# One block of a streaming encoder on one core: attention with ScalarE and VectorE in program order, takes set aside between the scores and Exp, other filler shares and weights loaded further ahead

## The chip, the core and the metric

The kernel runs on one core of one Trainium2 chip. The core has five engines that run their own instruction streams: TensorE (PE; its weight loads are shown apart as PEld), VectorE (DVE), ScalarE (ACT), GpSimd (POOL) and SyncE (SP, which here only issues DMA transfers). The metric is the device time of one launch in microseconds.

## The reference, cut to what matters

```python
D_MODEL = 1024; SEQ = 1024; ATT_HEADS = 8; ATT_HEAD_DIM = 64
CHUNK = 64; LEFT_CHUNKS = 8          # own chunk and 8 chunks before it
def mixer(h, ...):
    proj = h @ w_in
    q, k, v, xr, yr, g_att, g_rec = jnp.split(proj, idx, axis=-1)
    att = chunked_attention(q, k, v, rel_bias) @ w_att_o
    xr = causal_depthwise_conv(xr, conv_w, conv_b)
    rec = (rg_lru(xr, ...) * jax.nn.gelu(yr)) @ w_rec_o
    merged = jax.nn.sigmoid(g_att) * att + jax.nn.sigmoid(g_rec) * rec
    return merged @ w_out
def chunked_attention(q, k, v, rel_bias):   # per head, per chunk of queries
    scores = einsum(q, k_band) * 64**-0.5 + bias[rel]   # invalid keys masked
    return einsum(softmax(scores), v_band)
x = sandwich(x, ffn1, ...); x = sandwich(x, mix, ...); x = sandwich(x, ffn2, ...)
```

The block is a feed-forward half, this mixer and a second feed-forward half. Everything is float32. The kernel gets float32 products from three products of rounded parts: a value is split into a high part (`wh`, `k1h`) and the remainder (`wl`, `k1l`), and high × high, low × high and high × low are summed.

## The kernel before, in words

Only the attention stage matters here; it runs from about 1046 to 1361 us of the profiled span, between the recurrent branch and the merge. Its work is 64 units, in this order: four pairs of heads, two heads each, eight blocks of 128 queries. We call them unit 0 to 63. A unit's window has one to five blocks of 128 keys: in each head, the first query block sees one, the next two, and from the fifth on five. So units 0, 8, 16, ... are the narrow ones.

A unit goes through these steps (lines of the kernel before):

- S, the scores: PE writes a window of up to 640 columns into PSUM (two products up to 512 columns, L1675; four when it is wider, L1681).
- VectorE adds the bias and takes the row maximum in one instruction (L1686), then negates it (`nmx`, L1689). ScalarE does Exp with the row sum (L1690), VectorE the reciprocal (`ri`, L1691), ScalarE the division, a multiplication by `ri` (L1692).
- T, the transposes: PE turns the probabilities (`ptr`, L1700). ScalarE copies the high part out of PSUM (`tt`, L1704), VectorE makes the low part (L1705).
- V, the values: PE multiplies by v (`pvo`, L1718). After every second unit ScalarE and VectorE take the result out: o copy (L1728), two adds (L1729, L1730), `atth` (L1731) and `attl` (L1732).

PE's order is written out by hand: in step i come S of unit i+1, half of the step's filler, V of unit i−1, T of unit i, and the other half of the filler. In the text, "after unit n's scores" means that step. A filler is a product of a projection that is needed later: while pair p is worked on, q and k of pair p+1 are projected (`pproj`, L1552, 24 products of 512 tokens for each half of the tokens), the second half of v (`vproj`, L1616), and the attention's gate (`g_att`, 48 products for 128 channels, with tanh at L1633 and a store to memory). `GATES` says how many gate blocks each pair gets. `SHARE` says how much filler a unit gets by its window's width, and `begin` turns the weight of a pair's fillers into a rate.

A block of a projection, 24 products (48 for v), ends in one PSUM bank. Projections use two banks in turn (`psM`, bufs=2), so block n+2 may only start when what was taken out of block n has been read. These "takes" are left in a list, `left`, and `settle` runs them off later:

- q: ScalarE copies a scaled high part (L1575) and VectorE makes the difference (L1576), once for each of the two heads.
- k: ScalarE casts `k0h` (L1591), VectorE makes `k0l` (L1592), ScalarE casts the other half of `k0h` (L1596), and the same for `k1h`, `k1l`.
- v: ScalarE copies the high part (L1623), VectorE the difference (L1624). A gate: one tanh on ScalarE.

Before, only PE is in written order inside the attention. A scheduler orders ScalarE's and VectorE's instructions by when it estimates that they can run. `settle()` stands three times in each step and takes one item; when a block of a projection ends, `settle(99)` empties the list. Weights come by SP's DMA queue as `raw`, are cast by ScalarE to `wh` (L151), and GpSimd makes `wl`; they are prepared one unit of the plan ahead (`Weights(specs, ahead=1)`).

Of the kernel before, what the change touches and what calls it, by code (L numbers as in the profile page):

```python
# [23 lines left out]
P = 128  # L24
# [14 lines left out]
SHARE = (3, 4, 4, 5, 5)  # L39
LEFT = 40.0  # L40
GATES = (2, 0, 2, 4)
# [7 lines left out]
def kernel(  # L49
# [1449 lines left out]
    def att_phase(hh, hl, wts0, tg_dram, n_ga):  # L1499
        att_h, att_l = [], []  # L1500
        with (
# [11 lines left out]
            def v_w(half, i):  # L1513
                c0 = C_V + half * 256
                return prep(
                    w_in[i * 512 : (i + 1) * 512, c0 : c0 + 256].rearrange("(k p) n -> p k n", p=P), [P, 4, 256], nc.gpsimd
                )

            specs = {("v", 0, 0): partial(v_w, 0, 0), ("v", 0, 1): partial(v_w, 0, 1)}

            def spec_qk(p):
                specs["q", p] = partial(prep_cols, w_in, C_Q + p * P, eng=nc.gpsimd)
                specs["k", p] = partial(prep_cols, w_in, C_K + p * P, eng=nc.gpsimd)

            def spec_ga(n):
                specs["ga", n] = partial(prep_cols, w_in, C_GA + n * P, eng=nc.gpsimd)

# [6 lines left out]
            for p in range(4):  # L1534
                for kind, n in plan[p]:
                    if kind == "qk":
                        spec_qk(n)
                    elif kind == "ga":
                        spec_ga(n)
                    else:  # L1540
                        specs["v", 1, 0] = partial(v_w, 1, 0)
                        specs["v", 1, 1] = partial(v_w, 1, 1)
            wts = Weights(specs, ahead=1)

# [15 lines left out]

            def settle(n=1):
                for _ in range(min(n, len(left))):
                    left.pop(0)()

            def qk(p, out_t):
# [3 lines left out]
                for sh in range(2):  # L1569
                    sl = slice(sh * 512, (sh + 1) * 512)  # L1570
                    pj = yield from pproj(src["q", p], sh)
                    settle(99)

# [10 lines left out]
                for sh in range(2):  # L1584
                    sl = slice(sh * 512, (sh + 1) * 512)
                    pj = yield from pproj(src["k", p], sh)
                    settle(99)

# [15 lines left out]
            def vproj(half, out_t):  # L1604
                vt = []
                for sp in range(4):
                    settle(99)
                    pv = bank("pv")
                    for j in range(2):
                        tk = slice((2 * sp + j) * P, (2 * sp + j + 1) * P)  # L1610
                        dst = pv[:, j * 256 : (j + 1) * 256]
                        for k in range(KB):
                            wh, wl = wts["v", half, k // 4]
                            kk = k % 4
                            for i, (a, b) in enumerate(((hh, wh), (hh, wl), (hl, wh))):
                                nc.tensor.matmul(  # L1616
                                    dst, a[k][:, tk], b[:, kk, :], start=k == 0 and i == 0, stop=k == KB - 1 and i == 2
                                )
                                yield 0.5
                    t = t4("vt", F32R)  # L1620
                    t5 = t.rearrange("p (a q d) -> p a q d", q=4, d=HD)
                    src = pv.rearrange("p (a i d) -> p a i d", i=2, d=HD)
                    nc.scalar.copy(t5[:, :, 0::3, :], src)  # L1623
                    nc.vector.tensor_tensor(t5[:, :, 1:3, :], src, t5[:, :, 0::3, :].bitcast(F32), op=ALU.subtract)  # L1624
                    vt.append(t)
                out_t[half] = vt

            def g_att(n):
                for sh in range(2):
                    pj = yield from pproj(wts["ga", n], sh)  # L1630
                    settle(99)
                    tg = tmp[0].tile([P, 512], F32, tag="v", bufs=1, name=nm("tga"))
                    nc.scalar.activation(tg, pj, AF.Tanh, scale=0.5)  # L1633
                    nc.sync.dma_start(tg_dram[n * P : (n + 1) * P, sh * 512 : (sh + 1) * 512], tg)
                    yield 1.0
# [24 lines left out]
            def scores(u):  # L1660
# [27 lines left out]
                )  # L1688
                nc.vector.tensor_scalar(nmx, mx, -1.0, None, op0=ALU.mult)  # L1689
                nc.scalar.activation(pe[:, :w], pe[:, :w], AF.Exp, bias=nmx, accum_out=sm)  # L1690
                nc.vector.reciprocal(ri, sm)  # L1691
                nc.scalar.activation(pe[:, :w], pe[:, :w], AF.Copy, scale=ri)  # L1692
                return pe

            def probs_t(u, pe):
# [3 lines left out]
                for i in range(nk):  # L1699
                    nc.tensor.transpose(pt[:, i * P : (i + 1) * P], pe[:, i * P : (i + 1) * P], ident)  # L1700
                tt = tmp[0].tile([P, 5, 2, P], F32R, tag="tt", bufs=2, name=nm("tt"))
                src = pt[:, :w].rearrange("p (b n) -> p b n", n=P)
                hi, lo = tt[:, :nk, 0, :], tt[:, :nk, 1, :]
                nc.scalar.copy(hi, src)  # L1704
                nc.vector.tensor_tensor(lo, src, hi.bitcast(F32), op=ALU.subtract)  # L1705
                return tt

            def values(u, tt):
# [8 lines left out]
                for i in range(nk):  # L1717
                    nc.tensor.matmul(  # L1718
                        dst, vslice(p, h, kb0 + i), tt[:, i, :, :].rearrange("p a n -> p (a n)"),
                        start=i == 0, stop=i == nk - 1,  # L1720
                    )
                if qb % 2 == 1:
                    ah, al = atts[p]
# [5 lines left out]
                    nc.vector.tensor_tensor(o32[own], o32[own], pv[own, :, 0, :], op=ALU.add)  # L1729
                    nc.vector.tensor_tensor(o32[own], o32[own], pv[own, :, 1, :], op=ALU.add)  # L1730
                    nc.scalar.copy(ah[own, cols], of[own])  # L1731
                    nc.vector.tensor_tensor(al[own, cols], of[own], ah[own, cols].bitcast(F32), op=ALU.subtract)  # L1732

            def filler(p):
# [10 lines left out]

            with tc.manual_schedule(engines={PE_ENGINE}):
                load_bias(0)
                for _ in qk(0, qkt):
                    pass
                settle(99)  # L1750
                pe_next = scores(units[0])
                for _ in vproj(0, vts):
                    pass
                prev = None
# [11 lines left out]
                def drain():  # L1766
# [3 lines left out]
                    credit = 0.0  # L1770
                    settle(99)
# [8 lines left out]
                for i, u in enumerate(units):  # L1780
                    share = rate * SHARE[window(u[2])[1] - 1]
                    if i + 1 < len(units):
                        n = units[i + 1]
                        if n[1] == 0 and n[2] == 0:
                            drain()
                        pe_after = scores(n)
                        if n[1] == 0 and n[2] == 0:
# [7 lines left out]
                    settle()  # L1795
                    pe_next = pe_after
                    fill(share * 0.5)
                fill(LEFT * 0.4)
                values(*prev)
                drain()  # L1800
# [574 lines left out]
```

## Time and profile before

| | us |
|---|---|
| median of three runs | 2141.08 (2138.83 to 2143.11) |
| profiled execution, its own time | 2139.32 |
| its span in the trace | 2137.5 |
| PE busy | 2109.2, 99% of the span |
| DVE busy | 1393.7, 65% |
| ACT busy | 1049.2, 49% |
| attention: 1046 to 1361 | 315.00, PE busy 309.56 of it |

A line of an instruction group reads: line, engine, operation, output tile <- input tiles, shapes, number of instructions | busy us in all, mean ns of one | idle us of the engine just before them, and what ended most of it. A line of waits reads: the waiting engine, tile and line, what ended the wait, then the total in us, the number of waits and the longest.

### The profile page before, as it was taken

The page shows a single profiled execution, that of the slowest core. Times are in us where ns is not written, and L with a number is a line of the kernel's source. Part 1 is how long each engine was busy: PE and PEld are TensorE (multiplying, and loading weights), DVE is VectorE, ACT ScalarE, POOL GpSimd, SP SyncE. Part 2 cuts the span into 40 slices and gives each one's busy share as a digit, 9 for nine tenths or more (in the row PEclk, how much of TensorE's full clock was granted, in tenths as well). Part 3 has the DMA queues.
Part 4 walks back from the last instruction along what each step waited for, and adds up shares of the span by engine and source line. Part 5 has one row for each costly group of instructions (what it writes and reads, how often), then busy time and mean ns, then how long its engine had stood idle before and what let it go on. Part 6 is the DMA issues. An engine that isn't in the chain of part 4 may idle for free.

```text
span 2137.5 us, 26970 instructions
## 1 busy us (share of the span) xinstructions
PE 2109.2 (99%) x9877; PEld 1749.1 (82%) x9877; DVE 1393.7 (65%) x1878; ACT 1049.2 (49%) x1672; POOL 667.9 (31%) x490
## 2 busy tenths in 40 slices
PE   7999999999999999999999999999999999999998
PEld 5888888888888878888898888888888888888877
DVE  7766886567667687787346666586776655546466
ACT  5433333334357687854357777446343333334443
POOL 1168985422104110100122110002088874422102
PEclk9999999999999999999999999999999999999999
DMA  9457774469776232447611113457167653449465
GB/s 324 115 183 260 262 254 150 128 227 350 279 255 209 73 112 91 136 140 276 238 46 56 46 43 110 148 201 257 65 209 263 236 202 109 128 171 325 164 225 188
DMA packets 263085, 387.74 MB, mean 181 GB/s; under 512 B 17920, under 2 KB 163496, under 8 KB 262952
## 3 DMA queue, kind: packets, MB, share of 16 engines
q1 hardware_dynamic: 250032, 339.79, 47.5%
q10 hardware_dynamic: 12920, 46.23, 5.6%
q8 instruction: 77, 1.26, 0.2%
q14 instruction: 56, 0.46, 0.1%
HBM read 280.58 MB, written 108.52 MB: 182 GB/s over the span
## 4 chain that ended last, share of the span: by engine, by line
PE 87%; DVE 6%; ACT 3%; DMA 2%; issue 1%; SPq 1%; POOL 0%; DVEq 0%; ACTq 0%; POOLq 0%
PE px L992 10%; PE pv L992 8%; PE pj L1552 7%; PE pj L508 6%; PE psX L730 6%; PE psX L731 6%; PE psX L732 6%; PE pj L509 6%; PE pj L510 6%; PE psZ L731 3%; PE psZ L730 3%; PE psZ L732 3%; PE px L1412 2%; PE pv L1616 2%; PE px L1899 2%; PE psY L731 1%
## 5 line engine op out<-in xcount | busy, mean ns | idle before, releaser
L151 ACT CAST dh<-rawd 128x1024 fp32r<-128x1024 f32 x154 | 160.5, 1053 | 202.2 <-PE pv L992 54.0
L721 DVE TENSOR_TENSOR wm<-raw,wm 128x512 fp32r<-128x512 f32 x152 | 163.7, 1080 | 134.3 <-ACT wm L720 129.3
L154 DVE TENSOR_TENSOR dh<-rawd,dh 128x1024 fp32r<-128x1024 f32 x130 | 164.7, 1271 | 124.5 <-ACT dh L151 122.1
L508 PE MATMUL pj<-hh,wh 128*128 128x512 f32 x546 | 215.2, 394 | 0.0
L509 PE MATMUL pj<-hl,wh 128*128 128x512 f32 x546 | 212.8, 390 | 0.0
L510 PE MATMUL pj<-hh,wl 128*128 128x512 f32 x546 | 212.8, 390 | 0.0
L992 PE MATMUL px<-dh,dh 128*128 128x512 f32 x608 | 187.5, 390 | 1.4 <-DVE dh L154 1.4
L992 PE MATMUL pv<-dh,dh 128*128 128x512 f32 x528 | 162.7, 389 | 0.0
L154 POOL TENSOR_TENSOR wl<-raw,wh 128x1024 fp32r<-128x1024 f32 x20 | 48.3, 2422 | 295.4 <-ACT wh L151 249.8
L992 PE MATMUL px<-dh 128*128 128x512 f32 x352 | 137.7, 391 | 0.2 <-ACT dh L151 0.2
L930 POOL TENSOR_TENSOR act<-act,act 128x512 f32<-128x512 f32 x54 | 86.5, 1602 | 160.8 <-DMA act<-act 113.9
L992 PEld LDWEIGHTS px<-dh,dh 128*128 128x128 f32 x608 | 114.0, 188 | 25.8 <-DVE dh L154 2.1
L508 PEld LDWEIGHTS pj<-hh,wh 128*128 128x128 f32 x546 | 102.5, 188 | 23.5 <-issue 1.8
L510 PEld LDWEIGHTS pj<-hh,wl 128*128 128x128 f32 x546 | 102.5, 188 | 21.5
L509 PEld LDWEIGHTS pj<-hl,wh 128*128 128x128 f32 x546 | 102.6, 188 | 20.7 <-DVE hl L364 0.3
L992 PEld LDWEIGHTS pv<-dh,dh 128*128 128x128 f32 x528 | 98.9, 188 | 21.1 <-DVE dh L154 0.7
L730 PE MATMUL psX<-hs,wm 128*128 128x512 f32 x296 | 115.5, 390 | 0.1
L730 PE MATMUL psX<-hh,wm 128*128 128x512 f32 x296 | 115.3, 389 | 0.1
L732 PE MATMUL psX<-hs,wm 128*128 128x512 f32 x296 | 115.2, 389 | 0.0
L731 PE MATMUL psX<-hs,wm 128*128 128x512 f32 x296 | 115.2, 389 | 0.0
L732 PE MATMUL psX<-hh,wm 128*128 128x512 f32 x296 | 115.2, 389 | 0.0
L731 PE MATMUL psX<-hl,wm 128*128 128x512 f32 x296 | 115.1, 389 | 0.0
(362 smaller groups left out, 5485.8 us busy)
## 6 DMA issues: line engine op xcount, KB each, us to landing
rawa<-in_w_ada_dram SPq DMA_DIRECT2D x56, 512.0 KB, 6.5
rawd<-acts SPq DMA_DIRECT2D x88, 256.0 KB, 4.4
rawd<-downs SPq DMA_DIRECT2D x88, 256.0 KB, 5.0
raw<-in_w_in_dram SPq DMA_DIRECT2D x44, 512.0 KB, 4.0
raw<-in_ffn_w_gu_dram SPq DMA_DIRECT2D x43, 512.0 KB, 5.4
sr<-in_ffn_w_gu_dram SPq DMA_DIRECT2D x39, 512.0 KB, 6.3
act<-act SPq DMA_DIRECT2D x37, 512.0 KB, 5.5
acts<-act ACTq DMA_DIRECT2D x36, 512.0 KB, 4.0
```

Of the source, the lines that this page charges most:

```text
L151: nc.scalar.copy(hi, raw)
L154: (eng or nc.vector).tensor_tensor(lo, raw, hi.bitcast(F32), op=ALU.subtract)
L508: nc.tensor.matmul(dst, wh[:, kk, :], xhk[:, sl], start=first, stop=False)
L509: nc.tensor.matmul(dst, wh[:, kk, :], xlk[:, sl], start=False, stop=False)
L510: nc.tensor.matmul(dst, wl[:, kk, :], xhk[:, sl], start=False, stop=last)
L721: nc.vector.tensor_tensor(t[:, 1], src, t[:, 0].bitcast(F32), op=ALU.subtract)
L730: nc.tensor.matmul(dst, t[:, 0, kk, :], xh, start=first and kk == 0, stop=False, skip_group_check=True)
L731: nc.tensor.matmul(dst, t[:, 0, kk, :], xl, start=False, stop=False, skip_group_check=True)
L732: nc.tensor.matmul(dst, t[:, 1, kk, :], xh, start=False, stop=last and kk == 3, skip_group_check=True)
L930: nc.gpsimd.tensor_tensor(o, p, q, op=op)
L992: nc.tensor.matmul(dst, a_[:, 0, tk], w_[:, 1, :], start=first and n == 0, stop=last and n == 2, skip_group_check=True,)
L1552: nc.tensor.matmul(d, a[:, k, :], b[k][:, sl], start=k == 0 and i == 0, stop=k == KB - 1 and i == 2)
```

## The change

ScalarE and VectorE join PE in written order during attention. The code therefore says where each of their instructions goes:

- `aside` stands between `nmx` and Exp of the unit whose scores were just issued. It runs off up to three items of `left` for windows of more than three blocks, else two. A weight cast that is due takes the place of two of them.
- What is still in the list goes when the next block of a projection ends (`settle()` is now "all").
- The takes of v and the tanh of a gate go into `left` too; before, they ran as the block ended.
- The division is a generator step (`divide`): `ri`, and the division itself behind the high part of the transposes. The transposes' low part and the values' two halves are steps as well.
- The class `Queued` loads the weights of the unit four ahead in the plan and casts those two ahead.
- `LEFT`, the filler kept for the end, falls from 40 to 18, and `begin` divides by another total: pairs 1 and 2 no longer leave out one unit's share.

```diff
-LEFT = 40.0
+LEFT = 18.0
...
+            class Queued:
...
+                def load(self, n):
+                    while self.loaded < min(n, len(self.order)):
+                        key = self.order[self.loaded]
+                        src, shape = specs[key]
+                        raw = self.raws[key] = wpool.tile(shape, F32, tag="raw", bufs=3, name=nm("raw"))
+                        nc.sync.dma_start(raw, src.rearrange("(k p) n -> p k n", p=P))
+                        self.loaded += 1
...
+                def __getitem__(self, key):
+                    n = self.order.index(key)
+                    if n > self.asked:
+                        self.asked = n
+                        self.load(n + 4)
+                        for k in self.order[: n + 1]:
+                            self.cut(k)
+                        if n + 2 < len(self.order):
+                            casts.append((step[0] + 1, partial(self.cut, self.order[n + 2])))
+                    return self.got[key]
...
-            def settle(n=1):
+            def settle(n=99):
                 for _ in range(min(n, len(left))):
                     left.pop(0)()
+
+            def aside(n):
+                if casts and casts[0][0] <= step[0]:
+                    casts.pop(0)[1]()
+                    n -= 2
+                settle(max(n, 0))
...
                 nc.vector.tensor_scalar(nmx, mx, -1.0, None, op0=ALU.mult)
+                aside(3 if nk > 3 else 2)
                 nc.scalar.activation(pe[:, :w], pe[:, :w], AF.Exp, bias=nmx, accum_out=sm)
+                return pe, w, sm, ri
+
+            def divide(got):
+                pe, w, sm, ri = got
                 nc.vector.reciprocal(ri, sm)
+                yield
                 nc.scalar.activation(pe[:, :w], pe[:, :w], AF.Copy, scale=ri)
-                return pe
+                yield
...
-            with tc.manual_schedule(engines={PE_ENGINE}):
+            with tc.manual_schedule(engines={PE_ENGINE, mybir.EngineType.DVE, mybir.EngineType.Activation}):
...
-                    tot = sum(SHARE[window(b)[1] - 1] for b in range(SB)) * 2 - SHARE[4]
+                    tot = sum(SHARE[window(b)[1] - 1] for b in range(SB)) * 2 + {0: -SHARE[4], 3: SHARE[4]}.get(p, 0)
...
+                        got = scores(n)
+                        after = divide(got)
...
                     fill(share * 0.5)
+                    out_ = iter(())
                     if prev is not None:
-                        values(*prev)
-                    settle()
-                    prev = (u, probs_t(u, pe_next))
-                    settle()
-                    pe_next = pe_after
+                        out_ = values(*prev)
+                        next(out_)
+                    turned = probs_t(u, pe)
+                    next(turned)
+                    if after:
+                        next(after)
+                    next(out_, None)
+                    next(turned)
+                    tt = next(turned)
+                    if after:
+                        next(after)
+                    next(out_, None)
+                    prev = (u, tt)
                     fill(share * 0.5)
```

Where the instructions go shows in the order in which each engine gets them. In these rows a number behind a name tells tiles apart; the text ahead says which unit is meant. Line numbers of the changed kernel are higher by some 40 to 60.

ScalarE, before, around unit 24: the k casts of the second half of pair 2's k (`pj_1600_9798`), whose bank the second v block needs. `pe_1628` is unit 24, `pe_1611` unit 23.

```order
L1591 CAST k0h_1580_9713<-pj_1600_9798 64x512
L1692 ACTIVATE pe_1611_9854<-pe_1611_9854,ri_1615_9862 128x640
L1704 CAST tt_1618_9896<-ptr_1617_9890 128x5x128
L1731 CAST atth_1561_9638<-o32_1616_9881 64x256
L1596 CAST k0h_1580_9713<-pj_1600_9798 64x512
L1591 CAST k1h_1582_9715<-pj_1600_9798 64x512
L1690 ACTIVATE pe_1628_9937,sm_1631_9942<-pe_1628_9937,nmx_1630_9941 128x128
L1596 CAST k1h_1582_9715<-pj_1600_9798 64x512
```

ScalarE, after: the same casts (bank `pj_1610_9819`). `pe_1650` is unit 26, `pe_1639` unit 25.

```order
L1750 ACTIVATE pe_1639_9975<-pe_1639_9975,ri_1643_9981 128x256
L1793 CAST atth_1565_9643<-o32_1647_10005 64x256
L1635 CAST k0h_1584_9719<-pj_1610_9819 64x512
L1640 CAST k0h_1584_9719<-pj_1610_9819 64x512
L1743 ACTIVATE pe_1650_10024,sm_1653_10029<-pe_1650_10024,nmx_1652_10028 128x384
L1635 CAST k1h_1586_9721<-pj_1610_9819 64x512
L1640 CAST k1h_1586_9721<-pj_1610_9819 64x512
L1763 CAST tt_1659_10061<-ptr_1658_10057 128x2x128
```

The casts that stood around unit 24's Exp now stand around unit 26's. VectorE at these two places, before:

```order
L1592 TENSOR_TENSOR k0l_1581_9714<-pj_1600_9798,k0h_1580_9713 64x512
L1730 TENSOR_TENSOR o32_1616_9881<-o32_1616_9881,pvo_1607_9827 64x256
L1686 ISA pe_1628_9937,mx_1629_9940<-sc_1627_9936,bw_1528_9524 128x128
L1686 ISA mx_1629_9940 128x1
L1705 TENSOR_TENSOR tt_1618_9896<-ptr_1617_9890,tt_1618_9896 128x5x128
L1732 TENSOR_TENSOR attl_1562_9639<-o32_1616_9881,atth_1561_9638 64x256
L1689 TENSOR_SCALAR nmx_1630_9941<-mx_1629_9940 128x1
L1592 TENSOR_TENSOR k1l_1583_9716<-pj_1600_9798,k1h_1582_9715 64x512
```

and after:

```order
L1794 TENSOR_TENSOR attl_1566_9644<-o32_1647_10005,atth_1565_9643 64x256
L1738 ISA pe_1650_10024,mx_1651_10027<-sc_1649_10023,bw_1532_9532 128x384
L1738 ISA mx_1651_10027 128x1
L1741 TENSOR_SCALAR nmx_1652_10028<-mx_1651_10027 128x1
L1636 TENSOR_TENSOR k0l_1585_9720<-pj_1610_9819,k0h_1584_9719 64x512
L1636 TENSOR_TENSOR k1l_1587_9722<-pj_1610_9819,k1h_1586_9721 64x512
L1748 RECIPROCAL ri_1654_10030<-sm_1653_10029 128x1
```

Both low parts of k now stand behind unit 26's bias-and-maximum (`L1738 ISA`) and `nmx`. PE after these scores of unit 26 (`sc_1649`), after the change; `pv_1656` is the second v block, which goes into the bank of `pj_1610`:

```order
L1727 MATMUL sc_1649_10023<-k1l_1418_9009,q1_1372_8847 128x384
L1659 MATMUL pv_1623_9904<-wh_1599_9761,hh_166_966 128x256
L1659 MATMUL pv_1623_9904<-wl_1600_9762,hh_166_966 128x256
L1659 MATMUL pv_1623_9904<-wh_1599_9761,hl_174_974 128x256
L1659 MATMUL pv_1656_10046<-wh_1552_9594,hh_159_959 128x256
```

Three products stand between the scores and that block. The second place is unit 5 (`pe_1406` before, `pe_1410` after) and unit 6 on VectorE, with the differences of pair 1's q. Before:

```order
L1576 SCALAR_TENSOR_TENSOR q1_1368_8841<-pj_1372_8848,q1_1368_8841 64x512
L1705 TENSOR_TENSOR tt_1404_8973<-ptr_1403_8968,tt_1404_8973 128x4x128
L1686 ISA pe_1406_8984,mx_1407_8989<-sc_1405_8983,bw_1326_8450 128x640
L1686 ISA mx_1407_8989 128x1
L1689 TENSOR_SCALAR nmx_1408_8990<-mx_1407_8989 128x1
```

and after:

```order
L1765 TENSOR_TENSOR tt_1408_8978<-ptr_1407_8972,tt_1408_8978 128x4x128
L1738 ISA pe_1410_8990,mx_1411_8995<-sc_1409_8989,bw_1326_8450 128x640
L1738 ISA mx_1411_8995 128x1
L1741 TENSOR_SCALAR nmx_1412_8996<-mx_1411_8995 128x1
L1620 SCALAR_TENSOR_TENSOR q1_1372_8847<-pj_1374_8850,q1_1372_8847 64x512
```

The difference for the second head, `q1`, moves from ahead of unit 5's bias-and-maximum to behind its `nmx`; the next block, `pj_1420`, which takes the same bank, has its first product as the third filler behind unit 5's scores. The third place is PE at unit 47. Before, its scores (`sc_1875`) are followed at once by V and T:

```order
L1681 MATMUL sc_1875_11065<-k1l_1583_9716,q1_1536_9542 128x320
L1718 MATMUL pvo_1871_11040<-tt_1873_11052,vt_1642_10010 128x256
L1718 MATMUL pvo_1871_11040<-tt_1873_11052,vt_1665_10127 128x256 x2
L1718 MATMUL pvo_1871_11040<-tt_1873_11052,vt_1682_10221 128x256 x2
L1700 MATMUL ptr_1882_11091<-ident_69,pe_1866_11019 128x128 x5
```

and after:

```order
L1733 MATMUL sc_1877_11054<-k1l_1587_9722,q1_1540_9548 128x320
L1590 MATMUL pj_1873_11025<-hh_162_962,wl_1778_10597 128x512
L1590 MATMUL pj_1873_11025<-hh_163_963,wh_1777_10596 128x512
L1590 MATMUL pj_1873_11025<-hl_171_971,wh_1777_10596 128x512
L1590 MATMUL pj_1873_11025<-hh_163_963,wl_1778_10597 128x512
L1590 MATMUL pj_1873_11025<-hh_164_964,wh_1777_10596 128x512
L1590 MATMUL pj_1873_11025<-hl_172_972,wh_1777_10596 128x512
L1590 MATMUL pj_1873_11025<-hh_164_964,wl_1778_10597 128x512
L1778 MATMUL pvo_1874_11030<-tt_1876_11043,vt_1655_10045 128x256
```

Seven fillers now stand between the scores and V.

More of the change, by code (lines that the diff above doesn't have):

```diff
@@ L1540, in att_phase, with __init__, cut @@
                     else:
-                        specs["v", 1, 0] = partial(v_w, 1, 0)
-                        specs["v", 1, 1] = partial(v_w, 1, 1)
-            wts = Weights(specs, ahead=1)
+                        specs["v", 1, 0] = v_w(1, 0)
+                        specs["v", 1, 1] = v_w(1, 1)
+            class Queued:
+                def __init__(self):
+                    self.order = list(specs)
+                    self.raws, self.got = {}, {}
+                    self.loaded, self.asked = 0, -1
+                def load(self, n):
[5 more added lines that the diff above has]
+                        self.loaded += 1
+                def cut(self, key):
+                    if key in self.got:
+                        return
+                    raw = self.raws.pop(key)
+                    hi, lo = (wpool.tile(specs[key][1], F32R, tag=t, bufs=4, name=nm(t)) for t in ("wh", "wl"))
+                    split(raw, hi, lo, nc.gpsimd)
+                    self.got[key] = hi, lo
+                def __getitem__(self, key):
[8 more added lines that the diff above has]
+                    return self.got[key]
+            casts, step = [], [0]
+            wts = Queued()
             def pproj(w, sh):
@@ L1630, in g_att, with take_g @@
                     pj = yield from pproj(wts["ga", n], sh)
[L1631 to L1634, printed above, removed]
+                    settle()
+                    def take_g(pj=pj, sh=sh):
+                        tg = tmp[0].tile([P, 512], F32, tag="v", bufs=1, name=nm("tga"))
+                        nc.scalar.activation(tg, pj, AF.Tanh, scale=0.5)
+                        nc.sync.dma_start(tg_dram[n * P : (n + 1) * P, sh * 512 : (sh + 1) * 512], tg)
+                    left.append(take_g)
                     yield 1.0
@@ L1721, in values @@
                     )
+                yield
                 if qb % 2 == 1:
@@ L1744, in weight_of @@
                 return sum({"qk": 96.0, "v": 96.0, "ga": 48.0}[k] for k, _ in plan[p])
-            with tc.manual_schedule(engines={PE_ENGINE}):
+            with tc.manual_schedule(engines={PE_ENGINE, mybir.EngineType.DVE, mybir.EngineType.Activation}):
                 load_bias(0)
[L1748 to L1753, printed above, removed]
+                wts.load(3)
+                for n, _ in enumerate(qk(0, qkt)):
+                    settle(1)
+                    if n in (20, 50):
+                        wts.cut(wts.order[n // 50])
+                settle()
+                got = scores(units[0])
+                for n, _ in enumerate(vproj(0, vts)):
+                    settle(1)
+                    if n in (20, 100):
+                        wts.cut(wts.order[2 + n // 100])
+                    if n == 8:
+                        for _ in divide(got):
+                            pass
+                settle()
                 prev = None
@@ L1780, in att_phase @@
                 for i, u in enumerate(units):
+                    step[0] = i
                     share = rate * SHARE[window(u[2])[1] - 1]
+                    pe, after = got[0], None
                     if i + 1 < len(units):
                         n = units[i + 1]
[L1784 removed]
+                        fresh = n[1] == 0 and n[2] == 0
+                        if fresh:
                             drain()
[L1786 to L1787 removed]
+                        got = scores(n)
+                        after = divide(got)
+                        if fresh:
                             begin(n[0])
[L1789 removed]
+                    else:
+                        aside(3)
                     fill(share * 0.5)
+                    out_ = iter(())
                     if prev is not None:
[L1792 to L1796 removed]
+                        out_ = values(*prev)
[11 more added lines that the diff above has]
+                    prev = (u, tt)
                     fill(share * 0.5)
                 fill(LEFT * 0.4)
[L1799 removed]
+                for _ in values(*prev):
+                    pass
                 drain()
```

38 lines of the change are left out of this document (22 added, 16 removed).

## The prediction

> **What bounds the kernel now.** I read the page's busy shares and chain first, then the attention stretch, the only place where instructions change order: its busy times, TensorE's waits, the chain there, and the instruction groups of ScalarE and VectorE.
>
> ```profile
> PE 2109.2 (99%) x9877; PEld 1749.1 (82%) x9877; DVE 1393.7 (65%) x1878; ACT 1049.2 (49%) x1672; POOL 667.9 (31%) x490
> PE 87%; DVE 6%; ACT 3%; DMA 2%; issue 1%; SPq 1%; POOL 0%; DVEq 0%; ACTq 0%; POOLq 0%
> ```
>
> TensorE (PE) is busy for 99% of the span and carries 87% of the chain. ScalarE or VectorE matter only where PE waits for them. The stretch 1046 to 1361 us is attention:
>
> ```profile
> 1046.00:1361.00 315.00, 309.56 (x1826) 272.71 (x1825) 173.49 (x458) 205.51 (x414) 52.60 (x49) 1.00 0.21 65
> PE pvo L1718 <- DVE tt L1705: 3.4, 6, 1.1
> PE ptr L1700 <- ACT pe L1692: 0.9, 1, 0.9
> PE pj L1552 <- ACT k1h L1596: 0.7, 1, 0.7
> PE pj L508 <- ACT tga L1633: 0.4, 1, 0.4
> ```
>
> PE stands still for 315.00 − 309.56 = 5.4 us of 315; the four rows of its waits (total, times, longest) add to the same 5.4. So the most that a better order can give back here is 5.4 us, 0.25% of the run. VectorE is busy 55% and ScalarE 65%: they have room, if they are handed the right instruction at the right time.
>
> The chain gives PE's steps (start, us, what):
>
> ```profile
> 1068.09 23.08 PE pv L1616 x192
> 1100.65 0.59 PE sc L1681 x4
> 1101.24 1.61 PE pj L1552 x7
> 1108.15 0.55 PE ptr L1700 x5
> 1112.51 0.60 PE pvo L1718 x5
> ```
>
> A filler product for q, k or a gate costs 0.23 us, one for v 0.12, the scores S of a full unit 0.59, its transposes T 0.55, its values V 0.60.
>
> **The change, part by part.** All instruction counts stay. What moves is the order on ScalarE and VectorE, the fillers' share per step, and the weights' loads.
>
> *Removed idle.* The three V, T and k waits sit mostly at units 31 and 47, which have no fillers before; now each has some between S, V and T (the order shows seven at unit 47). The tanh's 0.4 goes too, as the last products now stand between. I take the whole 5.4 as the gain; the least is 0, if new V and T waits take its place.
>
> *Weights further ahead.* The loads are issued earlier on SP's queue, where the tanh stores and bias loads stand behind them. Three raw buffers were cast units ago when the fourth load comes. One landing is quick against a projection of 48 fillers (11 us):
>
> ```profile
> raw<-in_w_in_dram SPq DMA_DIRECT2D x44, 512.0 KB, 4.0
> ```
>
> I price this at nothing, from 0 to one landing (+4.0, at most once, if a raw buffer is still held).
>
> *The division behind the transposes' high part.* T waits for the division of its own unit, which is issued one unit earlier. At full width it delays by one high part, 0.68, and has over a step of fillers left: nothing as to T. It does delay the takes queued behind it.
>
> *The takes in program order: the large term.* All filler blocks share two PSUM banks, so block n+2 starts when the last take of block n has read its bank. Before, the scheduler put takes where ScalarE and VectorE were free. Now up to three stand between nmx and Exp of a unit, so those on VectorE wait behind the bias-and-maximum of the scores just issued, and the rest on ScalarE behind Exp, high part and division. The first product of the new block meets that queue on PE, which runs in order as well: everything behind it waits. The durations, ScalarE then VectorE:
>
> ```profile
> L1690 ACT ACTIVATE pe<-pe,nmx 128x640 f32<-128x640 f32 x32 | 26.6, 831 | 28.6 <-DVE nmx L1689 28.2
> L1692 ACT ACTIVATE pe<-pe,ri 128x640 f32<-128x640 f32 x32 | 26.6, 830 | 1.4 <-DVE ri L1691 1.2
> L1704 ACT CAST tt<-ptr 128x640 fp32r<-128x640 f32 x32 | 21.8, 682 | 1.6 <-PE ptr L1700 1.3
> L151 ACT CAST wh<-raw 128x1024 fp32r<-128x1024 f32 x18 | 18.9, 1050 | 15.6 <-DMA raw<-in_w_in_dram 6.4 <-PE pj L1552 4.7 <-PE pv L1616 3.8
> L1731 ACT CAST atth<-o 64x256 fp32r<-64x256 f32 x32 | 12.9, 404 | 5.0 <-DVE o L1730 4.6
> L1690 ACT ACTIVATION_READ_ACCUMULATOR pe<-pe,nmx 128x1 f32 x64 | 12.0, 187 | 0.0
> L1728 ACT COPY o<-pvo 64x256 f32<-64x256 f32 x32 | 11.7, 366 | 1.1 <-PE pvo L1718 0.4
> L1575 ACT ACTIVATE q<-pj 64x512 fp32r<-64x512 f32 x16 | 9.5, 592 | 7.9 <-PE pj L1552 4.5 <-DVE q L1576 3.2
> L1692 ACT ACTIVATE pe<-pe,ri 128x384 f32<-128x384 f32 x8 | 4.9, 617 | 0.5 <-DVE ri L1691 0.5
> L1690 ACT ACTIVATE pe<-pe,nmx 128x384 f32<-128x384 f32 x8 | 4.9, 618 | 2.6 <-DVE nmx L1689 2.6
> L1591 ACT CAST k1h<-pj 64x512 fp32r<-64x512 f32 x8 | 4.7, 584 | 0.1
> L1596 ACT CAST k0h<-pj 64x512 fp32r<-64x512 f32 x8 | 4.6, 579 | 5.9 <-DVE k0l L1592 5.8
> L1704 ACT CAST tt<-ptr 128x256 fp32r<-128x256 f32 x8 | 2.9, 365 | 1.2 <-PE ptr L1700 1.2
> ```
>
> ```profile
> L1686 DVE CUSTOM_DVE_ANT_0 pe<-sc,bw 128x640 f32<-128x640 f32 x32 | 26.2, 820 | 1.7 <-PE sc L1681 1.1
> L1732 DVE TENSOR_TENSOR attl<-o,atth 64x256 fp32r<-64x256 f32 x32 | 16.8, 525 | 1.8 <-ACT atth L1731 1.0
> L1576 DVE SCALAR_TENSOR_TENSOR q<-pj,q 64x512 fp32r<-64x512 f32 x16 | 11.0, 689 | 9.2 <-ACT q L1575 9.0
> L1689 DVE TENSOR_SCALAR nmx<-mx 128x1 f32<-128x1 f32 x64 | 9.6, 150 | 1.6
> L1592 DVE TENSOR_TENSOR k1l<-pj,k1h 64x512 fp32r<-64x512 f32 x8 | 5.6, 694 | 4.1 <-ACT k1h L1591 4.0
> L1686 DVE CUSTOM_DVE_ANT_0 pe<-sc,bw 128x384 f32<-128x384 f32 x8 | 4.4, 553 | 0.5 <-PE sc L1675 0.4
> ```
>
> The idle 5.8 in the k0h row, ended by VectorE's k0l, shows that a bank's takes go one after the other. The starting point, from the time line before unit 26's values:
>
> ```profile
> 1199.15 0.34 PE L1675 MATMUL sc<-k1l,q 128*128 128x384 f32 x1
> 1199.32 0.28 PE L1616 MATMUL pv<-wl,hh 128*128 128x256 f32 x1
> 1199.40 0.41 ACT L1731 CAST atth<-o 64x256 fp32r<-64x256 f32 x1 [0.31 <-DVE o L1730]
> 1199.53 0.56 DVE L1686 CUSTOM_DVE_ANT_0 pe<-sc,bw 128x384 f32<-128x384 f32 x1 [0.16 <-PE sc L1675]
> ```
>
> The next product issues at 1199.32; call that moment 0. The bias-and-maximum starts at 0.2; atth ends at 0.5.
>
> Unit 26, where PE reaches the second v block with its fourth filler, at 3 × 0.12 = 0.36. VectorE: attl to 1.0, maximum to 1.55, nmx (with a read-out of the accumulator, estimated at half of ScalarE's 0.19) to 1.8, k0l to 2.45; ScalarE: k0h's other half to 3.05, Exp with its read-out to 3.85, k1h to 4.45; VectorE: k1l to 5.15; ScalarE: k1h's other half to 5.75. PE waits 5.4.
> Unit 10 (a gate's second block): the same to Exp at 3.9, then high part 4.25, division 4.85, k1h 5.45, k1l 6.1, k1h's other half 6.7. PE is there after six fillers, one V, two T and two fillers, 1.38 + 0.12 + 0.22 + 0.46 = 2.2: waits 4.5.
> Unit 42: only k1l and k1h's other half are left: 1.8 + 0.7 + 0.6 = 3.1, against 0.46: 2.7 (rounded up).
> Unit 5: maximum and nmx to 1.2, q's difference to 1.95, against 0.46: 1.5.
> Unit 6: a weight cast and a q copy ahead put Exp at 1.4 to 2.4; high part, division, q copy, difference: 5.2; five handovers at an estimated 0.1: 5.7, against 1.61 + 0.60 + 0.55 + 0.92 = 3.7: 2.0.
> Units 22 and 38: like unit 5, but the weight cast (1.05) and q copy one unit earlier push the o copy, high part, division, atth and so attl about 1.2 later: 3.0 and 2.8 (bounds 1.7 and 1.5, without that push).
> Units 23 and 40: nmx 1.2, k0l 1.95, then k0h, k1h, Exp, o copy, high part, division, atth, k1h's other half in a row on ScalarE to 6.95, against 3.9 and 4.3: 3.0 and 2.65. Unit 8: 0.15.
>
> Sum: 5.4 + 4.5 + 2.7 + 1.5 + 2.0 + 3.0 + 2.8 + 3.0 + 2.65 + 0.15 = 27.7 us. Without handovers and pushes it is some 21; with handovers half as long again some 31. Elsewhere (tanh and v takes) the list is taken a whole step early: nothing.
>
> The profiled execution took 2139.3 us: 2139.3 − 5.4 + 27.7 = 2161.6, say 2162, since the median (2141.08) is 1.8 higher.
>
> **The rivals.**
> *Clock.* At the start of the run (window, its length, PE, PEld, DVE, ACT and POOL busy, granted clock):
>
> ```profile
> 14.00:16.00 2.00, 1.41 (x9) 0.78 (x7) 1.66 (x4) 0.62 (x1) 0.00 (x0) 1.00 1.20 292
> 16.00:18.00 2.00, 0.70 (x5) 0.57 (x5) 1.65 (x6) 1.77 (x3) 0.00 (x0) 1.00 1.16 304
> 18.00:20.00 2.00, 2.00 (x7) 1.28 (x6) 1.12 (x2) 2.00 (x5) 0.00 (x0) 0.51 1.11 350
> 20.00:22.00 2.00, 2.00 (x7) 1.63 (x6) 1.87 (x4) 0.61 (x3) 0.00 (x0) 0.64 1.18 306
> ```
>
> After 1.9 us of idle in four the clock fell to 0.51 and 0.64: 2.00 × 0.49 + 2.00 × 0.36 = 1.7 us lost. In attention, with waits up to 1.1, it stayed at 1.00. Waits of 4.5 and 5.4 us may bring it down twice: + 3.4, 2165; at six places + 10, 2172. Against: the short waits are spread over 300 us. [...]
>
> *Half absorbed.* A PE that waits gives the other engines time to catch up. If the later wait of each pair (units 6, 23, 40: 7.65) goes, the pushes at 22 and 38 too (2.6), and attl is done before the scores at 10, 26 and 42 (3.0), 14.5 remain: 2148. Against: the blocking takes stand behind the maximum of scores issued after the wait, so they cannot run ahead.
>
> *Faster.* The takes come free in time, as tanh's and v's do, if ScalarE and VectorE run nearly a step ahead of PE; then only the 5.4 shows: 2134. It decides where the ten waits together stay under 5.4, that is 0.5 each instead of 2.8. Against: a take behind the maximum of scores just issued cannot come before 1.95, and PE asks at 0.4 in four places.
>
> *The order does nothing.* ScalarE and VectorE end up in an order as good as before, and gain and new waits cancel: 2139 to 2141.
>
> **How the numbers follow.** The sum as worked out: 0.66. Clock falling at the long waits: 0.12. Half absorbed: 0.12. Faster: 0.06. Nothing: 0.04. A difference under 0.2% (4.3 us) can't be told here. Slower is 0.66 + 0.12 + 0.12 = 0.90. The range goes from the half absorbed case, 2147, to just under the clock's worst, 2171; the sum's bounds 21 and 31 give 2155 and 2165 inside it.
>
> **What the changed profile would show.** PE's waits in attention rise from 5.4 to about 28 us, with the filler's first product (pj or pv) waiting for the k casts (about 18, longest 5.4 at unit 26) and for q's differences on VectorE (about 9); the V waits for the low part vanish; all other stages keep their length. If the filler waits are below 5, the forecast is wrong; so it is if PE runs in attention at a clock under 1.00 for long, or if a raw load holds a cast up.

## The result, and the profile after

The changed kernel takes 2163.8 us (median of 4 runs, 2162.58 to 2165.7) against 2141.17 us for the kernel before, a ratio of 1.0108 (95% interval 1.0096 to 1.0119). The forecast was 2162, range 2147 to 2171. The profiled execution took 2163.96 us, its span is 2162.2.

The page after, busy shares and chain:

```profile
PE 2115.4 (98%) x9877; PEld 1754.5 (81%) x9877; DVE 1383.5 (64%) x1878; ACT 1047.4 (48%) x1672; POOL 668.1 (31%) x490
PE 83%; DVE 6%; ACT 4%; DMA 2%; POOL 2%; issue 2%; SPq 0%; DVEq 0%; POOLq 0%; ACTq 0%
```

PE's share of the chain falls from 87% to 83%. The attention stretch (window, length, PE, PEld, DVE, ACT and POOL busy, granted clock) and PE's waits in it (total, times, longest):

```profile
1046.00:1385.00 339.00, 316.35 (x1841) 279.01 (x1841) 170.24 (x457) 204.03 (x412) 55.14 (x50) 0.98 0.20 63
PE pj L1590 <- ACT k1h L1640: 8.6, 3, 4.0
PE pv L1659 <- ACT k1h L1640: 7.5, 2, 5.0
PE pj L1590 <- DVE q L1620: 6.5, 4, 1.9
```

The waits for V and T are gone. In their place stand nine waits, 22.6 us, all at the first filler of a new block, for the last k cast or the last q difference. The nine, in order of time (start, us, instruction, and in brackets the idle ahead of it and what ended it):

```profile
1112.73 0.50 PE L1590 MATMUL pj<-hh,wh 128*128 128x512 f32 x1 [1.37 <-DVE q L1620]
1123.19 0.50 PE L1590 MATMUL pj<-hh,wh 128*128 128x512 f32 x1 [1.92 <-DVE q L1620]
1143.28 0.79 PE L1590 MATMUL pj<-hh,wh 128*128 128x512 f32 x1 [4.03 <-ACT k1h L1640]
1195.11 0.50 PE L1590 MATMUL pj<-hh,wh 128*128 128x512 f32 x1 [1.74 <-DVE q L1620]
1206.33 0.39 PE L1659 MATMUL pv<-wh,hh 128*128 128x256 f32 x1 [2.54 <-ACT k1h L1640]
1220.00 0.58 PE L1659 MATMUL pv<-wh,hh 128*128 128x256 f32 x1 [5.01 <-ACT k1h L1640]
1273.37 0.50 PE L1590 MATMUL pj<-hh,wh 128*128 128x512 f32 x1 [1.52 <-DVE q L1620]
1284.35 0.50 PE L1590 MATMUL pj<-hh,wh 128*128 128x512 f32 x1 [2.14 <-ACT k1h L1640]
1294.96 0.50 PE L1590 MATMUL pj<-hh,wh 128*128 128x512 f32 x1 [2.40 <-ACT k1h L1640]
```

They are units 5, 6, 10, 22, 23, 26, 38, 40 and 42, the places of the forecast (the tenth, 0.15 at unit 8, isn't there). Each costs PE about 0.15 more than its bracket: at unit 26 the product ahead issued at 1214.71 and this one at 1220.00, which is 5.29 less the usual 0.12, so 5.17. Counted like this the nine are 1.5, 2.1, 4.2, 1.9, 2.7, 5.2, 1.7, 2.3 and 2.6 us, 24.2 in sum.

At two of the waits the granted clock also fell, to 0.50. Windows behind units 10 and 26:

```profile
1142.00:1144.00 2.00, 0.72 (x2) 0.63 (x3) 0.61 (x1) 1.18 (x2) 0.61 (x1) 0.83 0.00 0
1144.00:1146.00 2.00, 2.00 (x6) 1.52 (x5) 0.00 (x0) 0.00 (x0) 0.00 (x0) 0.50 0.35 131
1146.00:1148.00 2.00, 2.00 (x12) 1.72 (x10) 0.85 (x3) 0.82 (x2) 0.00 (x0) 0.82 0.00 0
1220.00:1222.00 2.00, 2.00 (x9) 2.00 (x10) 0.00 (x0) 0.00 (x0) 0.00 (x1) 0.50 0.00 0
1222.00:1224.00 2.00, 2.00 (x11) 2.00 (x10) 0.43 (x1) 1.25 (x3) 0.00 (x0) 0.50 0.03 8
1224.00:1226.00 2.00, 2.00 (x12) 1.86 (x12) 0.42 (x1) 0.11 (x1) 0.00 (x0) 0.69 0.00 0
```

While PE is busy, the lost part is 0.36 + 1.00 + 0.36 = 1.7 us behind unit 10 and 1.00 + 1.00 + 0.62 = 2.6 us behind unit 26, 4.3 in sum.

### The profile page after: what moved, and what is told of

Its sections match the earlier page's. It is cut to its first block, busy times and chain, and to the rows that moved or that the text cites. A ratio compares the mean times of both kernels' runs of the same rounds, so it can differ in the third digit from the quotient of the medians.

```text
span 2162.2 us, 26991 instructions
## 1 busy us (share of the span) xinstructions
PE 2115.4 (98%) x9877; PEld 1754.5 (81%) x9877; DVE 1383.5 (64%) x1878; ACT 1047.4 (48%) x1672; POOL 668.1 (31%) x490
## 4 chain that ended last, share of the span: by engine, by line
PE 83%; DVE 6%; ACT 4%; DMA 2%; POOL 2%; issue 2%; SPq 0%; DVEq 0%; POOLq 0%; ACTq 0%
PE px L992 10%; PE pv L992 8%; PE pj L1590 7%; PE pj L508 6%; PE psX L730 6%; PE pj L509 6%; PE pj L510 6%; PE psX L731 6%; PE psX L732 6%; PE psZ L731 3%; PE psZ L732 3%; PE psZ L730 3%; PE pv L1659 2%; PE px L1986 2%; PE psY L731 1%
## 5 line engine op out<-in xcount | busy, mean ns | idle before, releaser
L508 PE MATMUL pj<-hh,wh 128*128 128x512 f32 x546 | 215.4, 395 | 0.0
L1590 PE MATMUL pj<-hh,wh 128*128 128x512 f32 x256 | 103.7, 405 | 15.1 <-ACT k1h L1640 8.6
```

Of the source, the lines that this page charges most:

```text
L508: nc.tensor.matmul(dst, wh[:, kk, :], xhk[:, sl], start=first, stop=False)
L1590: nc.tensor.matmul(d, a[:, k, :], b[k][:, sl], start=k == 0 and i == 0, stop=k == KB - 1 and i == 2)
```

## The experiments

Two theories were put against each other. A: takes stand too late in the written order, PE waits for banks, and the longest waits lower the clock. B: the cost lies elsewhere in the change. Times are medians; ratios are to the kernel before, run on the same chip (2140.8 to 2142.0 there). "Attention" below is the time from the first product of the first scores to the first product of the last values in the profiled execution, with 1.8 us (8 fillers at 0.23) added where LEFT is 18, since these fillers come behind the last values there: 291.8 before and 313.1 after, 21.3 longer.

**Empty the list at each place (e1_aside_all).**

```diff
-                settle(max(n, 0))
+                settle()
```

> The changed kernel, with the place between nmx and Exp emptying the whole list of takes instead of up to three. Theory A (PE waits for banks because takes stand too late in the order: 24 us at nine places, and 4 us more from a lower clock after the two longest): q's takes and all k casts come a unit earlier, the nine waits fall below 1 us in sum; since Exp now stands behind four k casts, the transposes of units 9 and 41 wait about 1.6 us each: about 2140 us, granted clock 1.00 in attention. Theory B (the cost lies in the new shares, the weights' loads or the division's place): 2155 us or more.

2145.94 us, ratio 1.0016 (1.0007 to 1.0025). PE's waits:

```profile
PE pvo L1778 <- DVE tt L1765: 7.9, 6, 2.6
PE pv L1659 <- ACT k1h L1640: 0.4, 1, 0.4
```

The bank waits fall from 22.6 to 0.4, as A says. The price was put too low: 7.9 us of waits for V, since Exp and all behind it now stand behind four k casts, and the clock still falls twice, at two of these waits (3.1 us).

**Only PE in written order (e2_pe_only).** The engine set of `manual_schedule` is `{PE_ENGINE}` again, the rest of the change stays.

> The changed kernel, with only PE in written order; the scheduler places ScalarE's and VectorE's instructions as before the change, everything else (shares, weights, aside, division) stays. Theory A: the bank waits go, 2134 to 2140 us. Theory B (shares, weights or the way the takes are left cost the time): 2155 us or more.

2137.71 us, ratio 0.9984 (0.9974 to 0.9993), faster than before. In its attention:

```profile
PE pvo L1778 <- DVE tt L1765: 2.0, 3, 1.2
PE ptr L1758 <- ACT pe L1750: 0.4, 1, 0.4
```

No bank wait is left. The shares, the weights and the deferred takes are not what cost the time; this written order on ScalarE and VectorE is. Theory B falls.

**Only the shares (e3_shares).** The kernel before with `LEFT = 18.0` and the new totals.

> The kernel before, with only LEFT = 18 and the new totals in begin, so that units 31 and 47 have fillers. Theory A: the idle at these units goes, 2.5 to 5.4 us of gain: 2136 to 2139 us. Theory B (the shares bring PE to the bank changes at worse moments): 2150 us or more, with waits of the fillers for k's casts or q's differences.

2141.48 us, ratio 0.9998 (0.9989 to 1.0008): no change.

```profile
PE pvo L1718 <- DVE tt L1705: 3.2, 4, 1.4
PE sc L1675 <- DVE mx L1686: 0.5, 1, 0.5
```

With two single waits more (0.7 for a k cast, 0.4 for a division) 4.8 us of waits, against 5.4 before. With fillers at units 31 and 47 the scheduler's order makes PE wait at other units: the longest wait, 1.4, now stands at unit 49. Both theories expected a difference and were wrong here.

**Two places with room for two takes (e4_two_places).**

```diff
-                    n -= 2
+                    n -= 0 if step[0] in (8, 24) else 2
```

> The changed kernel; only at the scores of units 9 and 25 a weight cast takes no place from the takes, so that two k takes go there. Theory A with the clock: unit 10's wait falls from 4.2 to about 0.9 and unit 26's from 5.2 to about 2.7, no wait is long enough to lower the clock (1.00 throughout attention), and the slow stretches behind them (4.3 us) go as well: 2163.8 - 3.3 - 2.5 - 4.3 = about 2154 us. Theory A without the clock (slow stretches come by chance): about 2158 us, the clock still under 1.00 somewhere in attention. The other seven waits stay as they were.

2158.25 us, ratio 1.0078 (1.0061 to 1.0095). Attention is 308.4, 4.7 less than after. Units 10 and 26 now wait 1.6 and 3.5 (idle in the trace; 0.9 and 2.7 were put), the other seven as in the changed kernel:

```profile
PE pj L1590 <- ACT k1h L1640: 6.1, 3, 2.4
PE pv L1659 <- ACT k1h L1640: 6.0, 2, 3.5
```

The clock did not stay up: it falls behind unit 26 and, unlike in the changed kernel (1.00 from 1294 to 1298), behind unit 42, where the wait is 2.4 in both:

```profile
1286.00:1288.00 2.00, 2.00 (x6) 1.54 (x5) 0.30 (x1) 0.84 (x2) 0.00 (x0) 0.50 0.14 55
```

So the waits moved as A says, though less, but my estimate that no wait here would be long enough to lower the clock failed.

**Takes first (e5_takes_first).** Takes before weight casts, all of them at each place, and k's four casts ahead of its two low parts:

```diff
-                if casts and casts[0][0] <= step[0]:
-                    casts.pop(0)[1]()
-                    n -= 2
-                settle(max(n, 0))
+                if left:
+                    settle()
+                elif casts and casts[0][0] <= step[0]:
+                    casts.pop(0)[1]()
...
+                    def cast_k(own, oth, pair, pj=pj, sl=sl):
+                        nc.scalar.copy(pair[0][own, sl], pj[own])
+                        nc.scalar.copy(pair[0][oth, sl], pj[own])
+                    def low_k(own, oth, pair, pj=pj, sl=sl):
+                        kh, kl = pair
+                        nc.vector.tensor_tensor(kl[own, sl], pj[own], kh[own, sl].bitcast(F32), op=ALU.subtract)
+                        nc.gpsimd.tensor_copy(kl[oth, sl], kl[own, sl].bitcast(F32))
+                    for f in (cast_k, low_k):
+                        for own, oth, pair in ((lo_, up, kt[0]), (up, lo_, kt[1])):
+                            left.append(partial(f, own, oth, pair))
```

> The changed kernel with all three engines in written order, but: the place between nmx and Exp always empties the list of takes, a weight cast goes there only when no takes wait, and of k's takes ScalarE's four casts come first and VectorE's two low parts behind them (before, they alternated). Theory A (only the place and the chain of the takes cost the time): q's and k's banks are free about 2.6 to 3.2 us after the scores of the unit before PE needs them, no filler waits, waits for V of under 2 us in sum, clock 1.00: 2134 to 2137 us, faster than the kernel before. Theory B (written order on ScalarE and VectorE costs time in itself, as it can't adapt): 2141 us or more, with waits of V or T in place of those of the fillers.

2133.35 us, ratio 0.9964 (0.9951 to 0.9976): 30 us under the changed kernel and faster than the kernel before. Its window, to set beside that of before:

```profile
1046.00:1361.00 315.00, 315.00 (x1864) 279.91 (x1863) 173.57 (x461) 205.74 (x415) 55.27 (x50) 1.00 0.22 70
```

PE is busy for all of it, at full clock. Attention is 284.1. This is the yardstick for the others: the kernel before loses 291.8 − 284.1 = 7.7 us to idle, the changed kernel 29.0, which is 24.2 of waits, 4.3 of clock and 0.5 unexplained.

**Each half of that alone (e9_place_only, e10_chain_only).** e9 has the first edit, e10 the second.

> The changed kernel with one of the two edits of e5_takes_first: the list of takes is emptied at each place and a weight cast goes there only when no takes wait; k's casts and low parts alternate as in the changed kernel. If the place is what matters: q's waits and the long k waits go; the alternating chain (about 4 us from the scores) still holds back Exp, so waits of V for the low part remain, less than the 7.9 us of e1_aside_all because no weight cast stands ahead of the chain, 3 to 6 us: 2138 to 2142 us. If the chain is what matters: above 2150 us.

> The other edit alone: k's four casts first and its two low parts behind them, the places limited to two or three and shared with weight casts as in the changed kernel. If the place is what matters: q's waits stay (7 us), those for k stay in sum about as long (low parts left over go at the end of a block, behind the transposes' and values' low parts), some 21 us of waits and one or two slow stretches of 1.7 us: about 2160 us. If the chain is what matters: k's waits go, about 2143 us.

e9: 2143.3 us, ratio 1.0006 (0.9997 to 1.0016), V waits 7.2 us and one bank wait of 0.3; a little above its forecast: the alternating chain holds back Exp almost as much as in e1, and the clock fell twice, 3.4 us in all. The second fall came behind this wait:

```profile
1271.60 0.85 PE L1778 MATMUL pvo<-tt,vt 128*128 128x256 f32 x5 [1.91 <-DVE tt L1765]
1274.00:1276.00 2.00, 2.00 (x6) 1.61 (x6) 1.24 (x5) 0.82 (x2) 0.45 (x1) 0.50 0.09 25
```

e10: 2158.39 us, ratio 1.0077 (1.0062 to 1.0092):

```profile
PE pj L1590 <- DVE q L1620: 6.6, 4, 1.9
PE pv L1659 <- DVE k1l L1639: 5.5, 2, 3.7
PE pj L1590 <- DVE k1l L1639: 3.8, 2, 2.4
PE pj L1590 <- ACT tga L1683: 2.5, 1, 2.5
```

18.4 us of bank waits stay, and the clock fell twice (0.55 from 1142 to 1144, 0.50 from 1216 to 1218; 3.4 us in all). So the places (how many takes, and that a weight cast pushes them on) carry most, some 20 us; the order inside k's takes is worth 10 more once the places are right (2143.3 to 2133.35), 3.4 of it the clock.

**One wait, two lengths (e6_late_one, e7_late_more).** e5 with nothing run off at the places of steps 23 and 24, or 23 to 25. The clock theory is A with the clock as in e4, that only a long wait lowers it; its rival, that the shorter of the two does too.

> The kernel of the run e5_takes_first, with one set of takes (the second half of pair 2's k) held back to unit 26's place: one bank wait of about 2.8 us at unit 26 and nothing else. [...]

> The same with these takes held back behind unit 26's Exp: one bank wait of 5 to 6 us at unit 26. Clock theory and rival alike: half clock for 3.4 to 6.8 us behind the wait, 1.7 to 3.4 us on top of it, so 6.7 to 9.4 us slower than e5_takes_first. If the clock has no part in the cost of the changed kernel: 5 to 6 us slower.

2138.5 us (0.9986; 0.9977 to 0.9995) and 2140.75 us (0.9992; 0.9983 to 1.0002), so 5.2 and 7.4 us above e5; attention 5.6 and 8.2 longer. Each has one wait, 3.7 and 5.6 in the trace, 3.9 and 5.7 by PE's issue. The first, and the windows behind it:

```profile
PE pv L1661 <- DVE k1l L1641: 3.7, 1, 3.7
1202.00:1204.00 2.00, 2.00 (x12) 2.00 (x11) 0.36 (x1) 0.76 (x2) 0.00 (x0) 0.50 0.04 8
1204.00:1206.00 2.00, 2.00 (x12) 1.92 (x11) 0.14 (x2) 0.60 (x2) 0.00 (x0) 0.65 0.00 0
```

1.00 + 0.70 = 1.7 lost, and 3.9 + 1.7 = 5.6 is what attention grew by. The clock's part of the cost is shown: only the place of these takes differs between these kernels. The clock theory and its rival are not told apart here, since the first wait came out at 3.7 and not at the 2.8 that was put. But length alone didn't decide: in e9 the clock fell to 0.50 behind 1.9 us, and in the changed kernel it was 1.00 behind 2.5 us at unit 23.

**The old shares on e5 (e8_old_shares).** `LEFT = 40.0` and the old totals.

> The kernel of the run e5_takes_first with the shares of before (LEFT = 40 and the old totals), so that units 31 and 47 have no fillers again. If those units are where the kernel before lost its V and T waits: about 2.5 us of waits come back there, 2.5 us slower than e5_takes_first. If the shares are worth nothing, as in e3_shares: the same time within 1 us.

2136.89 us, ratio 0.998 (0.9972 to 0.9989), 3.5 above e5.

```profile
PE pvo L1778 <- DVE tt L1765: 1.9, 2, 1.0
PE pj L508 <- DVE o L1791: 1.7, 1, 1.7
```

The two V waits stand in the steps right behind units 31 and 47, and the merge waits for the last values. With ScalarE and VectorE in a fixed, good order the shares are worth 3.5 us; with the scheduler's order (e3) they were worth nothing.

**A shorter lead for the weights on e5 (e11_weights).** Loads three ahead, casts one ahead.

> The kernel of e5_takes_first with weights loaded three units ahead of the plan and cast one ahead, instead of four and two. If the longer lead is worth nothing here: the same time within 1.5 us, no wait of a filler for a weight. If it is needed: waits of the fillers for wh or wl, 1 us or more each at some of the changes of a projection.

2143.31 us, ratio 1.0006 (0.9996 to 1.0015), 10 us above e5.

```profile
PE pv L1659 <- ACT wh L151: 2.9, 1, 2.9
PE pv L1659 <- POOL wl L154: 2.0, 1, 2.0
```

A third wait of this kind took 0.8, and the clock fell behind the first (0.50 from 1194 to 1200; 2.4 us). Where takes go first, a weight cast can be put off for several units. The longer lead pays for that; the run shortens loads and casts together, so which of the two is needed stays open.

**The division ahead of the high part, on e5 (e12_division).** Both steps of `divide` stand right behind T, so the division comes before the high part.

> The kernel of e5_takes_first with the division directly behind its reciprocal, ahead of the high part of the transposes, instead of behind it. If the division's place carries little: the high part comes 0.8 to 1.1 us later, the low part is still ready over a microsecond before V asks for it, and the time stays within 1.5 us of e5_takes_first (2133 to 2135 us). If it is the division's place that rid the changed kernel of the waits for V and T: V waits for the low part at several of the 64 units, 3 to 8 us slower, 2136 to 2141 us.

2173.26 us, ratio 1.0149 (1.0134 to 1.0163), 40 us above e5 and far outside both expectations. PE waits in the stretch 1046 to 1361, and a piece of the time line:

```profile
PE pvo L1778 <- DVE tt L1765: 18.7, 22, 2.7
PE pj L1590 <- DVE q L1620: 1.0, 1, 1.0
...
1110.23 0.83 ACT L1750 ACTIVATE pe<-pe,ri 128x640 f32<-128x640 f32 x1 [0.23 <-DVE ri L1748]
1111.08 0.59 ACT L1763 CAST tt<-ptr 128x512 fp32r<-128x512 f32 x1
1111.70 0.69 DVE L1765 TENSOR_TENSOR tt<-ptr,tt 128x512 fp32r<-128x512 f32 x1 [1.51 <-ACT tt L1763]
1112.31 0.81 DVE L1738 CUSTOM_DVE_ANT_0 pe<-sc,bw 128x640 f32<-128x640 f32 x1
1113.36 0.83 ACT L1743 ACTIVATE pe<-pe,nmx 128x640 f32<-128x640 f32 x1 [0.74 <-DVE nmx L1741]
1114.51 0.83 ACT L1750 ACTIVATE pe<-pe,ri 128x640 f32<-128x640 f32 x1 [0.23 <-DVE ri L1748]
...
1121.15 0.83 ACT L1750 ACTIVATE pe<-pe,ri 128x640 f32<-128x640 f32 x1 [0.23 <-DVE ri L1748]
```

The rows form a ring: division, high part, low part, next bias-and-maximum, Exp, next division, each behind the one before. From 1110.23 to 1114.51 it takes 4.3 us without any take or result to copy. PE's own step at full width is 0.59 + 2 × 1.61 + 0.60 + 0.55 = 5.0. An o copy (0.37), the adds and two q takes lift the next round to 6.6 (1114.51 to 1121.15), and then ScalarE and VectorE set the pace. Over the 64 units, VectorE takes up the scores 1.75 us behind their end on average, against 0.54 in e5. With the division behind the high part, the low part doesn't wait for it, so it is outside the ring. Attention, which runs on to 1393 here, is 38.7 longer than in e5: 29.4 by PE's issue in 32 waits (24.2 in the trace), 1.7 from one fall of the clock (0.99 from 1046 to 1361), and the rest, some 7.6, in delays of 0.25 or less, most of them at V.

## Why the prediction was right, point by point

- *What bounds.* Right: PE, and what it waits for. The other engines stayed at 64% and 48%.
- *Removed idle, −5.4.* The waits for V, T and the tanh went. Against e5 the kernel before lost 7.7 us, not 5.4: its eight waits ahead of the last values (the tanh's stands behind them) are 5.0 in the trace and, at some 0.15 more each by PE's issue, 6.2; the other 1.5 stay unexplained. The reason given was only half of it. Of the 5.0, 2.5 stand in the steps of units 31, 32, 47 and 48, and 2.3 at units 8, 24 and 40, which have fillers. Fillers at units 31 and 47 alone gave nothing (e3), and on a fixed order 3.5 us with the merge's wait (e8).
- *The takes, +27.7.* Mechanism and places right, measured 24.2. The size was off in two terms: units 22 and 38, put at 3.0 and 2.8, were 1.9 and 1.7, near the bounds of 1.7 and 1.5 that were given. The push of 1.2 us by a weight cast was not there; it was added although a bound spoke for the smaller value. The other seven are within 0.4. The 0.1 put for a handover at unit 6 was an estimate without a row; at unit 26 a handover between ScalarE and VectorE takes 0.03 to 0.04 (k1h ends at 1218.60, k1l starts at 1218.63). The lower bound of 21 doesn't follow from the terms: without the named handovers (0.5) and pushes (2.6) they make 24.6, close to what was measured.
- *Half absorbed, faster.* Neither came. The later waits of the pairs stayed (2.1, 2.7 and 2.3 at units 6, 23 and 40), and of what the first of these rivals took away only the pushes were missing.
- *Unit 26 in rows.* The product behind the scores issues at 1214.47. Expected, from there: nmx 1.8, k0l 2.45, k0h's other half 3.05, Exp 3.85, k1h 4.45, k1l 5.15, the other half 5.75. The time line:

```profile
1215.92 0.15 DVE L1741 TENSOR_SCALAR nmx<-mx 128x1 f32<-128x1 f32 x1
1215.99 0.67 DVE L1636 TENSOR_TENSOR k0l<-pj,k0h 64x512 fp32r<-64x512 f32 x1
1216.70 0.58 ACT L1640 CAST k0h<-pj 64x512 fp32r<-64x512 f32 x1 [1.26 <-DVE k0l L1636]
1217.29 0.61 ACT L1743 ACTIVATE pe<-pe,nmx 128x384 f32<-128x384 f32 x1
1218.02 0.58 ACT L1635 CAST k1h<-pj 64x512 fp32r<-64x512 f32 x1
1218.63 0.69 DVE L1636 TENSOR_TENSOR k1l<-pj,k1h 64x512 fp32r<-64x512 f32 x1 [1.97 <-ACT k1h L1635]
1219.36 0.58 ACT L1640 CAST k1h<-pj 64x512 fp32r<-64x512 f32 x1 [0.76 <-DVE k1l L1636]
```

  Ends at 1.6, 2.2, 2.8, 3.5 (Exp with its read-out of 0.19, which starts at 1217.81), 4.1, 4.85 and 5.5: the order of the forecast, 0.2 to 0.35 earlier. In part that is because an instruction can start before the one ahead has ended (k0l at 1215.99, nmx until 1216.07).
- *The clock.* Put as a rival with 0.12 and + 3.4 us; it came, with 4.3, at units 10 and 26, whose waits had been put at 4.5 and 5.4. Left out of the main sum, it was the step that failed; it made up for the 3.5 us by which the waits were overrated. That the number came within 2 us is in part luck: with the clock alone put right the forecast would have been about 2166, with the waits alone about 2158.5, both still inside the range. The 1.7 us put for one fall is what it cost in e6 and at unit 10; at unit 26 it cost 2.6. How long a wait must be was not shown: e9 fell to 0.50 behind a wait of 1.9 us in the trace.
- *Weights further ahead, nothing.* Right for this kernel, where no filler waits for a weight. e11 shows the cover: without the longer lead, takes going first would cost 10 us. The shorter lead on the changed kernel itself was not run.
- *The division, nothing.* Wrong in its reasoning. I asked only whether T gets its input in time. The division's place sets what VectorE's next instruction waits for, through the high and the low part; e12 prices it at 40 us on e5. How much it carries in the changed kernel itself wasn't run.
- *Net.* 27.7 − 5.4 = 22.3 forecast for attention; 24.2 + 4.3 − 7.7 + 0.5 = 21.3 there (the 0.5 is what was left over, so the sum closes by its making), and 22.6 between the medians. The profiled executions differ by 24.7 in span, mostly because the scores begin 5.05 us later after the change (1072.81 against 1067.76). Of that, 3.4 is the clock ahead of attention: it was granted at 0.57 from 16 to 24 us and again from 498 to 502, against 0.79 and 1.00 before. The late start doesn't make the changed kernel slow: e5's scores begin at 1073.53, and it is the fastest.

## What to carry to other kernels

When an engine is put in written order, follow each buffer that another engine needs to its last reader, and ask what stands ahead of that reader in its own queue, not whether the engine is idle on average. A helper task with slack (here a weight cast) must not take the place of one without (a take that frees a bank). And check the ring: in e12's program order the division stood between two instructions that wait for each other across engines and lengthened every round; at 4.3 to 6.6 us a round, against 5.0 for a step of the engine that bounds the kernel, the ring set the pace.

## What the runs showed of the hardware

- PE's clock fell to half at single waits of 4.0 and 5.0 us in the trace (the changed kernel, units 10 and 26), 3.5 (e4, unit 26), 3.7 (e6, e10) and 5.6 (e7), and at some waits of 1.9 to 2.9 us (e1, e4, e9, e10, e11, e12), but not at the 2.5 and 2.4 us of the changed kernel's units 23 and 42 (1.00 in the windows from 1206 to 1210 and 1294 to 1298). At unit 42 the same 2.4 us lowered it in e4 (0.50 from 1286 to 1288). What decided at such waits was not shown.
- The changed kernel was at 0.50 from 1143.31 to 1146.72 and from 1218.41 to 1225.23, so for 3.4 and 6.8 us, which cost 1.7 and 2.6 us of PE's busy time. In the other runs each fall in attention cost 1.4 to 1.7 us, or 2.4 to 2.7 (e7, e11).
- Ahead of attention the changed kernel's clock also fell without a long wait: it was 0.50 from 498.20 to 501.61, behind a stretch, 494 to 498, in which PE was idle for 0.35 us.
- The alternating takes of one bank, ScalarE, VectorE, ScalarE, took 4.0 us at unit 26 from k0l's start to the last cast's end, for five takes and Exp. Put as four casts and then two low parts, they let Exp and the banks come early enough that no wait was left (e5 against e9).
